# First loads in strict order, and the memory norm moved from the first to the second pass, in a two-layer encoder

## The chip, the cores and the metric

The kernel runs on all eight cores of one Trainium2 chip. Every core does the whole network for one of the eight batch elements, and no data passes between cores. The metric is device time in microseconds (us) of the slowest core. Cores 0 to 3 lie on one die, cores 4 to 7 on the other.

Executions come in two states. In the slow one a die, or both, shows a lower granted TensorE clock in the records, and the time is some per cent longer; the same kernel has both. One more disturbance turned up that this division into states doesn't catch: in some runs called fast, a *pair* of cores has a mean clock of 0.980 to 0.985 where the other cores have 0.992 and more, and the time is 12 to 28 us longer. The ratios on record count such runs as fast; each one is marked below.

Engine names: PE is TensorE (matmul), PEld its weight loads, DVE VectorE, ACT ScalarE, POOL GpSimd, SP SyncE. A name with q, as SPq, is an engine's sequencer, here the issue of a DMA.

## The reference, cut to what matters

```python
def rms_norm(x, g):
    y = x * lax.rsqrt(jnp.mean(x * x, axis=-1, keepdims=True) + EPS)
    return y * g

def swiglu(x, w_gate, w_up, w_down):
    return (jax.nn.silu(x @ w_gate) * (x @ w_up)) @ w_down

def reference(x, mem, ...):                  # x (8, 2048, 1024), mem (8, 256, 1024)
    for l in range(2):
        g = norm_g[l]
        h = swiglu(rms_norm(x, g[0]), ...)   # hidden width 2816: first FFN
        x = x + 0.5 * rms_norm(h, g[1])
        ...                                  # token mixer
        m = rms_norm(mem, mem_norm_g[l])     # the "memory norm"
        h = cross_attention(rms_norm(x, g[4]), m, ...)
        ...                                  # and a second FFN
    return x
```

The memory norm depends on `mem` alone, so it may be done at any time before the first cross-attention, some 600 us into the program. It is done once for both layers: they share the root mean square and differ in the gain.

## The kernel before: the parts that matter

A core's x is 2048 tokens in four blocks of 512 (x block 0 to 3, 2 MB each in fp32). An FFN makes two passes, each over two blocks: gate and up products first (11 pairs of hidden tiles), then the down-projection. The products are done with a seven-product Strassen scheme, for which VectorE makes sums of weights (tiles `SW`) and of inputs (tiles `TX`); in the down-projection these are `SDA` and `TS`. `ER` and `ss` are intermediate results, and `H` is the hidden result of a pair. Only the first two pairs of the first pass are done "plainly", with eight products in place of seven, because the input sums need x block 1, which isn't there yet. Weights come in panels of 256 KB through POOL's DMA queue (`SL<-wflat`), x and mem through SP's queue.

First loads and first products:

```python
k.dma("pool", ... CB ...)                       # a constant table
x_load(0, 2)                                    # x block 0, four DMAs
x_load(1, 4)                                    # x block 1, two DMAs, at once behind it
...                                             # panel 0 is issued when half of x block 1 is in:
reads=([("X", c, 1) for c in range(4)] if i == 0 else ())
...
for tb in tbs:                                  # plain products: block 0, pairs 0 and 1,
    for i in range(j0 // 2):                    # then block 1, pairs 0 and 1
        plain_pair(held[i], i, tb)
        if tb == tbs[1]:
            for nm in BLK:
                ws.release(held[i][nm])         # frees slots: the next panels can be issued
```

The rest of the first pass is a list of events at product steps (one step is eight matmuls of 128x512, about 1.7 us). x blocks 2 and 3 are issued from step 2, their norms come at steps 11.5 and 18.5, and the memory norm at step 21.5:

```python
if (l, f, hf) == (0, 0, 0):
    ev += [(XA + XD * n, "xload", ...) for n in range(8)]
    ev += [(XL[0], "xnorm", 2), (XL[1], "xnorm", 3), (XL[2], "mnorm", 0)]
```

```python
def mem_norm():
    k.later(None, writes=m32k, dma=("sp", [... m32 <- memT ...]))       # 1 MB
    k.later({"act": ... activation(out=msq, in_=m32, func=AF.Square)})  # one big square on ACT
    for c in range(8):
        stat_later(st, psk, MSQ[:, c, :], ..., n=MEM)                   # 8 matmuls: column sums
    rk_, use = rstd_later(...)                                          # ACT: Ln, then Exp(-0.5 *)
    for l in range(L):
        for c in range(8):                                              # 16 DVE operations
            ... scalar_tensor_tensor(out=MNL[l][:, c, :], in0=M32[:, c, :], scalar=gain, in1=R) ...
        ... DMA mscr[l] <- MNL[l] ...                                   # stored for the attention
```

The SwiGLU needs the function Silu on ACT, the norm needs Ln and Exp; this will matter.

The softmax here doesn't subtract the row's maximum and nothing guards it: scores larger than these inputs give would overflow.

## Time and profile before

| | before |
|---|---|
| time, the runs given at first | 2461.39 us median of 3 (2457.8 to 2772.29) |
| cores in the profiled run | 2434.2 to 2461.5 us, core 5 the slowest |
| PE busy, core 5 | 2373.9 us, 96% |
| first down-projection begins, by core | 171.2 us (core 6) to 190.5 us (core 3) |

The head of the profile's page, on core 5. The rows of digits are busy tenths in 40 slices of 61.5 us; PEclk is the granted clock in tenths.

```profile
span 2461.5 us, 35363 instructions; the slowest of 8 cores (2434.2 to 2461.5 us)
...
PE 2373.9 (96%) x11280; PEld 1094.8 (44%) x11280; DVE 1754.1 (71%) x2253; ACT 1229.2 (50%) x1757; POOL 352.6 (14%) x679
...
PE   6979999998999999999999999999999999999998
...
PEclk9989999999999999999999999999999999999999
```

What the reader is to see is that PE is the limit and that the only slices with a digit under 8 are the first (0 to 62 us) and the third (123 to 185 us). The view of waits tells what. It lists, for core 5 in the first 225 us, what PE stood for: the total, how often, and the longest, in us.

```profile
PE pp L350 <- ACT XN L930: 13.0, 4, 9.8
PE pp L350 <- ACT msq L2114: 11.3, 1, 11.3
PE pp L350 <- DMA SL<-wflat: 5.2, 2, 4.4
PE pp L350 <- ACT ER_76 L1282: 3.1, 1, 3.1
PE pp L350 <- DVE SW_80 L1260: 1.7, 1, 1.7
...
```

The first line is mostly the very start, where the first x has to land (9.8 us at one time). The second is the memory norm. The timeline of core 5 shows it; columns are start, duration, engine, line, operation and tiles, how many, and in brackets the idle time before and what ended it.

```profile
142.09 0.37 SPq L2112 DMA_DIRECT2D m_166<-memT  x1
...
162.47 1.91 ACT L2114 ACTIVATE msq<-m_166 128x2048 bf16<-128x2048 f32 x1 [13.32 <-DMA m_166<-memT]
...
164.63 1.65 PE L350 MATMUL pp<-msq,onesm 128*128 128x256 bf16 x7 [11.27 <-ACT msq L2114]
```

mem (its tile is `m_166`) is issued at 142.1 and lands 20 us later. ACT stands still for 13.3 us before the square (the bracket of its line): what is queued behind the square waits too, and PE with it for 11.3 us. In the view of windows the 20 us before and after the landing look like this (PE, PEld, DVE, ACT, POOL busy, then clock, DMA share, GB/s):

```profile
140.00:160.00 20.00, 13.33 (x62) 5.67 (x59) 10.68 (x13) 5.03 (x5) 2.63 (x5) 0.90 1.02 178
160.00:180.00 20.00, 15.31 (x63) 6.88 (x64) 9.25 (x14) 10.08 (x10) 0.00 (x0) 0.76 0.08 14
```

The DMA engines are full while mem lands, since weight panels go through them at the same time, and the clock is at 0.76 after the pause. The landing took 8.6 to 20.2 us over the cores, and the cores where it was long (0, 3, 4, 5 and 7: 14.6 to 20.2) are the cores that start their down-projection late (185.3 us and later).

### The profile page before, as it was taken

What the parts mean: (1) busy time and instruction counts of PE and PEld (TensorE: products, weight loads), DVE (VectorE), ACT (ScalarE), POOL (GpSimd) and SP (SyncE); (2) the same over time, 40 slices, a digit from 0 to 9 for tenths busy, and PEclk for the clock granted to TensorE, in tenths of its full rate; (3) what the DMA queues carried; (4) which work ended last, traced back from release to release, by engine and by line L of the source; (5) the groups of instructions that cost most, each with busy time, mean ns of one, the idle gap of its engine ahead of it and who ended that gap; (6) DMA issues with size and microseconds to landing.
All of it is one profiled execution on the core that took longest, in us unless ns stands there. A gap on an engine that the chain in (4) does not pass through costs nothing.

```text
span 2461.5 us, 35363 instructions; the slowest of 8 cores (2434.2 to 2461.5 us)
## 1 busy us (share of the span) xinstructions
PE 2373.9 (96%) x11280; PEld 1094.8 (44%) x11280; DVE 1754.1 (71%) x2253; ACT 1229.2 (50%) x1757; POOL 352.6 (14%) x679
## 2 busy tenths in 40 slices
PE   6979999998999999999999999999999999999998
PEld 2434444444454444444444444445444444444445
DVE  4656796566378888588679759836656878876765
ACT  3543553438667754365355345433227785634433
POOL 1111111112220011111111111111001101111210
PEclk9989999999999999999999999999999999999999
DMA  7755666758761167466666667675235204755954
GB/s 140 144 87 97 121 126 123 156 118 132 134 103 27 22 112 139 80 132 114 134 125 126 124 124 147 118 151 128 46 73 90 52 1 73 151 94 91 166 95 138
DMA packets 127684, 267.95 MB, mean 109 GB/s; under 512 B 15120, under 2 KB 25616, under 8 KB 127504
## 3 DMA queue, kind: packets, MB, share of 16 engines
q0 software_dynamic: 95760, 183.25, 47.1%
q1 hardware_dynamic: 31744, 82.44, 10.4%
q8 instruction: 96, 1.57, 0.3%
q14 instruction: 84, 0.69, 0.1%
HBM read 408.73 MB, written 35.91 MB: 181 GB/s over the span
## 4 chain that ended last, share of the span: by engine, by line
PE 85%; DMA 4%; DVE 4%; ACT 3%; issue 3%; SPq 1%; DVEq 0%; ACTq 0%; POOL 0%; POOLq 0%
PE pp L350 85%; DMA X<-xT 1%; DMA m_166<-memT 1%; DMA SL<-wflat 1%; SPq L1869 0%; DVE H L1284 0%; DMA mscr<-mnl_169 0%; ACT ER_76 L1282 0%; DMA slot_51<-wflat 0%; DMA slot_49<-wflat 0%; ACT rw L1087 0%; DMA YB<-YP_118 0%; ACT L1282 0%; DVE X L973 0%; ACT ER_77 L1282 0%
## 5 line engine op out<-in xcount | busy, mean ns | idle before, releaser
L350 PE MATMUL pp<-XH,SL 128*128 128x512 f16 x2192 | 493.9, 380 | 7.2 <-DMA SL<-wflat 5.2
L628 POOL DMA_DIRECT2D SL<-wflat x352 | 185.9, 531 | 1099.4 <-PE pp L350 807.9
L350 PEld LDWEIGHTS pp<-XH,SL 128*128 128x128 f16 x2192 | 213.8, 98 | 271.6 <-issue 19.1
L1401 ACT ACTIVATE X<-pp 128x512 f32<-128x512 f32 x112 | 66.9, 597 | 238.6 <-PE pp L350 232.1
L350 PE MATMUL pp<-TX_74,SL 128*128 128x512 f16 x688 | 163.1, 380 | 4.5 <-ACT ER_76 L1282 3.4
L350 PE MATMUL pp<-TX_72,SW_80 128*128 128x512 f16 x688 | 165.0, 382 | 1.8 <-DVE SW_80 L1260 1.7
L350 PE MATMUL pp<-XH,SW_79 128*128 128x512 f16 x688 | 163.8, 381 | 1.7 <-DVE ER_77 L1284 1.5
L350 PE MATMUL pp<-TX_73,SW_78 128*128 128x512 f16 x688 | 162.8, 379 | 0.9 <-DVE SW_78 L1260 0.9
L350 PE MATMUL pp<-XN,WQK 128*128 128x512 bf16 x512 | 121.2, 379 | 3.7 <-ACT VWO L1151 2.3
L930 ACT ACTIVATE XN<-X 128x512 bf16<-128x512 f32 x176 | 105.8, 638 | 35.6 <-DVE X L973 14.1
L1282 ACT ACTIVATE pp<-pp 128x1024 f32<-128x1024 f32 x86 | 86.7, 1008 | 40.1 <-PE pp L350 38.4
L1405 DVE TENSOR_TENSOR X<-pp,X 128x512 f32<-128x512 f32 x56 | 38.6, 690 | 95.1 <-PE pp L350 55.1
L350 PEld LDWEIGHTS pp<-TX_74,SL 128*128 128x128 f16 x688 | 66.5, 98 | 88.6 <-issue 10.3
L350 PEld LDWEIGHTS pp<-TX_72,SW_80 128*128 128x128 f16 x688 | 67.3, 98 | 85.2 <-issue 6.7
L350 PEld LDWEIGHTS pp<-XH,SW_79 128*128 128x128 f16 x688 | 67.1, 98 | 85.3 <-issue 6.9
L350 PEld LDWEIGHTS pp<-TX_73,SW_78 128*128 128x128 f16 x688 | 66.8, 98 | 83.5 <-issue 3.6
L1282 ACT ACTIVATE ER_77<-pp 128x1024 f32<-128x1024 f32 x61 | 62.2, 1020 | 55.5 <-PE pp L350 39.2
L1282 ACT ACTIVATE ss_81<-pp 128x1024 f32<-128x1024 f32 x60 | 61.2, 1020 | 53.3 <-PE pp L350 34.0
L1282 ACT ACTIVATE ER_75<-pp 128x1024 f32<-128x1024 f32 x62 | 63.2, 1020 | 44.8 <-PE pp L350 30.8
L1282 ACT ACTIVATE ER_76<-pp 128x1024 f32<-128x1024 f32 x61 | 62.2, 1020 | 45.9 <-PE pp L350 30.0
L945 DVE SCALAR_TENSOR_TENSOR XH<-X,cf_sb,rw 128x512 f16<-128x512 f32 x96 | 66.8, 746 | 20.8 <-PE pp L350 16.2
L350 PE MATMUL pp<-H,sdb 128*128 128x512 f16 (+1 forms) x352 | 78.8, 372 | 0.0
(663 smaller groups left out, 4603.4 us busy)
## 6 DMA issues: line engine op xcount, KB each, us to landing
SL<-wflat POOLq DMA_DIRECT2D x352, 256.0 KB, 5.4
xscr<-X SPq DMA_DIRECT2D x48, 512.0 KB, 4.0
X<-xscr SPq DMA_DIRECT2D x48, 512.0 KB, 4.9
WN_147<-wflat POOLq DMA_DIRECT2D x32, 352.0 KB, 6.0
X<-xT SPq DMA_DIRECT2D x20, 512.0 KB, 8.1
WSL<-wflat POOLq DMA_DIRECT2D x28, 352.0 KB, 11.1
WN_148<-wflat POOLq DMA_DIRECT2D x24, 352.0 KB, 7.1
wx_146<-wflat POOLq DMA_DIRECT2D x16, 352.0 KB, 6.7
```

What stands on the lines that cost most here:

```text
L350: self.q["pe"].append((waits, (lambda e: e.matmul(out, lhsT=l_, rhs=r_, start=st, stop=sp, skip_group_check=grp)), inc))
L628: self.k.dma("pool", lambda e, dst=dst, src=src: e.dma_start(out=dst, in_=src), "w%d" % idx, cost=1.6, reads=([("X", c, 1) for c in range( ...
L930: k.later({"act": lambda e, sap=sap, xap=xap: e.activation(out=sap, in_=xap, func=AF.Square)}, reads=[xk(c, tb)], writes=skeys)
L945: k.later({"dve": lambda e, c=c, oap=oap, xap=xap: e.scalar_tensor_tensor(out=oap, in0=xap, scalar=G(l, n, c), in1=R[st["r"]][:, :], op0=A ...
L1282: act = lambda o_, i_, fn, rk, wk, **kw: k.later({"act": lambda e: e.activation(out=o_, in_=i_, func=fn)}, reads=rk, writes=wk, cost={"act ...
L1401: cpy = lambda o_, b, wk, **kw: k.later({"act": lambda e: e.activation(out=o_, in_=P[b][:, 0:T], func=AF.Copy)}, reads=[("P", b)], writes= ...
L1405: k.later({"dve": lambda e: e.tensor_tensor(out=o_, in0=P[b][:, 0:T], in1=o_, op=ALU.add)}, reads=[("P", b)] + ok, writes=ok, **kw)
```

## The change

The intent is to give the opening a strict order of loads, so that the first product starts early and nothing that isn't wanted yet takes bandwidth, and to take the memory norm out of a stretch where its load comes late. x is also laid out by block in memory, so that a load of a block reads long runs. The core of the diff (cut are the layout of x, the constant table `CB`, which is now loaded late, the split of `plain_pair` into products and evacuation, six filler matmuls behind the first pair, and the squares of x block 1, which are now summed by eight matmuls instead of by VectorE and two):

```diff
-        x_load(0, 2)
-        x_load(1, 4)
+        for c in range(0, 8, 2):
+            x_part(0, c, 2)
+        ws.prefetch(4, [xk(4, 0)])                       # panels 0-3 behind 3/4 of x block 0
+        for c in range(0, 8, 2):
+            x_part(1, c, 2, w_key(2) if c == 0 else ())  # x block 1 behind panel 2
+        ws.prefetch(8, [xk(4, 1)])                       # panels 4-7 behind 3/4 of x block 1
+        for tb in (2, 3):
+            for c in (4, 6, 0, 2):
+                x_part(tb, c, 2, w_key(6) if (tb, c) == (2, 4) else ())   # x 2, 3 behind panel 6
...
-                    for tb in tbs:
-                        for i in range(j0 // 2):
+                    for i in range(j0 // 2):
+                        for tb in tbs:                   # pair 0: block 0, block 1; then pair 1
+                            made = plain_pair(held[i], i, tb)
...
+                        if i == 0:                       # third pair: its weight sums, early
+                            ps[j0 // 2] = Pair(l, f, hf, j0 // 2)
+                            ps[j0 // 2].sums()
...
-        XL = (11.5, 18.5, 21.5)
+        XL = (11.5, 18.5)
+        ML = (43.5, 59.5)
...
-                    ev += [(XA + XD * n, "xload", (2 + n // 4, (4, 6, 0, 2)[n % 4])) for n in range(8)]
-                    ev += [(XL[0], "xnorm", 2), (XL[1], "xnorm", 3), (XL[2], "mnorm", 0)]
+                    ev += [(XL[0], "xnorm", 2), (XL[1], "xnorm", 3)]
+                if (l, f, hf) == (0, 0, 1):              # second pass
+                    ev += [(ML[0], "mload", 0), (ML[1], "mnorm", 0)]
...
-                stat_later(st, psk, MSQ[:, c, :], msqk, c == 0, c == 7, n=MEM)
+                stat_later(st, psk, MSQ[:, c, :].unsqueeze(1).broadcast_to([128, 2, MEM]), msqk, c == 0, c == 7)
```

The norm's tiles move with it: from the place of x blocks 2 and 3, which is free in the first pass once those are normalised, to that of blocks 0 and 1, which is free in the second pass once those are spilled.

More of the change, by code (lines that the diff above doesn't have):

```diff
@@ L83, in to_phase, with pack_x @@
     return np.ascontiguousarray(a.reshape(a.shape[0], PW, NPH).transpose(0, 2, 1)).reshape(a.shape[0], S)
+def pack_x(x):
+    return np.ascontiguousarray(to_phase(np.ascontiguousarray(x.T)).reshape(8, 128, NTB, TB).transpose(2, 1, 0, 3))
 def from_phase(a):
@@ L616, in __init__, with prefetch, _issue @@
         self.wflat = None
-    def _issue(self):
+    def prefetch(self, n, gate):
+        while self.sched is not None and self.issued < n:
+            self._issue(gate)
+            gate = ()
+    def _issue(self, gate=()):
         i = self.issued
@@ L628, in _issue @@
         self.k.dma("pool", lambda e, dst=dst, src=src: e.dma_start(out=dst, in_=src), "w%d" % idx, cost=1.6,
-                   reads=([("X", c, 1) for c in range(4)] if i == 0 else ()), writes=keys)
+                   reads=gate, writes=keys)
         self.issued += 1
@@ L697, in build @@
     nc = bass.Bass("TRN2", target_bir_lowering=False)
-    xT = nc.dram_tensor("xT", [D, S], F32, kind="ExternalInput").ap()
+    xT = nc.dram_tensor("xT", [NTB, 128, 8, TB], F32, kind="ExternalInput").ap()
     memT = nc.dram_tensor("memT", [D, MEM], F32, kind="ExternalInput").ap()
@@ L785, in build @@
     TSR = sb("tsr", OFF_X + 30720, [NK - 9, TU], F16)
-    M32 = sb("m32", OFF_X + 32768, [8, MEM], F32)
-    MSQ = sb("msq", OFF_X + 40960, [8, MEM], BF16)
-    MNL = [sb("mnl%d" % i, OFF_X + 45056 - i * 4096, [8, MEM], BF16) for i in range(L)]
+    M32 = sb("m32", OFF_X, [8, MEM], F32)
+    MSQ = sb("msq", OFF_X + 8192, [8, MEM], BF16)
+    MNL = [sb("mnl%d" % i, OFF_X + 12288 - i * 4096, [8, MEM], BF16) for i in range(L)]
     WQK = AT(nc, "WQK", 32768, [8, 1024], BF16)
@@ L824, in program @@
         k.dma("sp", lambda e: e.dma_start(out=CF[:, :], in_=cfd), "c0", writes=[("CF",)])
-        k.dma("pool", lambda e: e.dma_start(out=CB[:, :], in_=cbd), "c1", writes=[("CB",)])
-        xv = xT.rearrange("(c p) t -> p c t", p=128)
+        k.t["hq"] = 4.0
         def x_part(tb, c, n, reads=()):
@@ L830, in x_part, with w_key @@
             k.dma("sp", lambda e: e.dma_start(out=X[:, lo // 1024, c:c + n, lo % 1024:lo % 1024 + TB],
-                                              in_=xv[:, c:c + n, lo:hi]), "xl%d_%d" % (tb, c),
+                                              in_=xT[tb, :, c:c + n, :]), "xl%d_%d" % (tb, c),
                   reads=reads, writes=[xk(q, tb) for q in range(c, c + n)], cost=0.9 * n)
-        def x_load(tb, n):
-            for c in range(0, 8, n):
-                x_part(tb, c, n)
-        x_load(0, 2)
-        x_load(1, 4)
+        def w_key(i):
+            return SLOTS16[i]((0, SLOT_ELEMS))[1]
+        for c in range(0, 8, 2):
[7 more added lines that the diff above has]
+                x_part(tb, c, 2, w_key(6) if (tb, c) == (2, 4) else ())
         k.op("dve", lambda e: e.memset(ONESM[:, :], 1.0 / 1024.0), writes=[("ONES",)])
@@ L845, in program @@
         k.op("dve", lambda e: e.memset(SGN[:, 1:2], -isq), writes=[("ONES",)])
-        CONST = [("CF",), ("CB",), ("ONES",)]
+        CONST = [("CF",), ("ONES",)]
+        CONSTB = CONST + [("CB",)]
         k.op("act", lambda e: e.activation(out=SS[0][:, 0:2], in_=ONES1[:, 0:2], func=AF.Ln), reads=[("ONES",)], writes=[("S", 0)],
@@ L909, in add @@
                     self.stack.append((sq, sqk))
-        stats = {}
+        stats, rks = {}, {}
         k.sqfree = list(range(7))
@@ L941, in prenorm @@
             stats[(l, n, tb)] = psk
+            rks[(l, n, tb)] = rk_
             for c in (4, 5, 6, 7, 0, 1, 2, 3) if n in (0, 6) and tb > 1 else range(8):
@@ L1215, in x_reload @@
             lo, hi = p * 2 * TB, (p + 1) * 2 * TB
-            src = xv[:, c, lo:hi] if (l, f) == (0, 0) and hf == 0 else xscr[:, c, lo:hi]
+            src = xT[2 * p:2 * p + 2, :, c, :].rearrange("t p n -> p t n") if (l, f) == (0, 0) and hf == 0 else xscr[:, c, lo:hi]
+            dst = X[:, p, c, :].rearrange("p (t n) -> p t n", t=2) if (l, f) == (0, 0) and hf == 0 else X[:, p, c, :]
             k.later(None, reads=[("XS", c, p)] + list(paced), writes=[xk(c, 2 * p), xk(c, 2 * p + 1)], dma=("sp", [
-                lambda e: e.dma_start(out=X[:, p, c, :], in_=src)], "xs%d_%d" % (p, c), 3.0))
+                lambda e: e.dma_start(out=dst, in_=src)], "xs%d_%d" % (p, c), 3.0))
         def ho_x(tb):
@@ L1473, in plain_pair @@
             lo, hi = tbr(tb)
-            tl = ((tb % 2) * TB, (tb % 2 + 1) * TB)
             tiles = [(q, r) for q in range(2) for r in "12"]
@@ L1482, in plain_pair, with plain_evac @@
                     k.mm(P[b][:, :], [(w.t[:, o:o + 128], xap, w.keys + xkeys)], b, start=(kk == 0), stop=(kk == 7))
+            return i, tb, bs
+        def plain_evac(i, tb, bs):
+            tl = ((tb % 2) * TB, (tb % 2 + 1) * TB)
             for q in range(2):
@@ L1494, in program @@
         RB = (2.2, 5.2, 7.2, 10.2, 14.2, 16.2, 18.2, 20.2)
-        XA, XD = 2.0, 1.7
-        XL = (11.5, 18.5, 21.5)
+        XL = (11.5, 18.5)
+        ML = (43.5, 59.5)
         MORE = 2
@@ L1511, in ffn @@
                 plain = nxt is None and hf == 1
+                ps = {}
                 j0 = 0
@@ L1520, in ffn @@
                         k.mm(P[b][:, :], [(ONESM[:, :], ALT[:, :], [("ONES",), stats[(0, 0, 0)]])], b)
-                    for tb in tbs:
-                        for i in range(j0 // 2):
-                            plain_pair(held[i], i, tb)
-                            if tb == tbs[1]:
-                                for nm in BLK:
-                                    ws.release(held[i][nm])
+                    for i in range(j0 // 2):
+                        for tb in tbs:
+                            made = plain_pair(held[i], i, tb)
+                            if (i, tb) == (0, 0):
+                                b = k.bank()
+                                for _ in range(6):
+                                    k.mm(P[b][:, :], [(ONESM[:, :], ALT[:, :], [("ONES",)])], b)
+                                k._check([rks[(0, 0, 1)]] + [q for kk in range(4) for q in XH(kk, tbr(1))[1]], [])
+                            plain_evac(*made)
+                        for nm in BLK:
+                            ws.release(held[i][nm])
+                        if i == 0:
+                            ps[j0 // 2] = Pair(l, f, hf, j0 // 2)
+                            ps[j0 // 2].sums()
                     token_sums(0, 2)
@@ L1530, in ffn @@
                 ev = [(7 * (i - i0) + first.get((i - i0, pr), off), pr, i) for i in range(i0, i1)
-                      for pr, off in (PLAN if i < i1 - 1 else PLANQ)]
+                      for pr, off in (PLAN if i < i1 - 1 else PLANQ) if i not in ps or pr not in ("in", "sum")]
                 end = 7 * (i1 - i0)
                 if (l, f, hf) == (0, 0, 0):
-                    ev += [(XA + XD * n, "xload", (2 + n // 4, (4, 6, 0, 2)[n % 4])) for n in range(8)]
-                    ev += [(XL[0], "xnorm", 2), (XL[1], "xnorm", 3), (XL[2], "mnorm", 0)]
+                    ev += [(XL[0], "xnorm", 2), (XL[1], "xnorm", 3)]
+                if (l, f, hf) == (0, 0, 1):
+                    ev += [(ML[0], "mload", 0), (ML[1], "mnorm", 0)]
                 if (l, f, hf) != (0, 0, 0) and not plain:
@@ L1567, in ffn @@
                 ev.sort(key=lambda x: x[0])
-                ps = {}
                 k.wide, k.lag = True, LAG
@@ L1576, in ffn @@
                         ps[i].last()
-                    elif pr == "xload":
-                        x_part(i[0], i[1], 2, tick())
                     elif pr == "xnorm":
@@ L1582, in ffn @@
                         k.bg = False
+                    elif pr == "mload":
+                        k.later(None, reads=tick(), writes=[("CB",)], dma=("pool", [lambda e: e.dma_start(out=CB[:, :], in_=cbd)], "c1", 1.6))
+                        mem_fetch(tick())
                     elif pr == "mnorm":
@@ L1702, in even_mixer @@
                 b = k.bank()
-                k.mm(P[b][:, :], [(CB[:, CB_CSC + j * 128:CB_CSC + (j + 1) * 128], CB[:, CB_FW:CB_FW + 512], CONST)], b)
+                k.mm(P[b][:, :], [(CB[:, CB_CSC + j * 128:CB_CSC + (j + 1) * 128], CB[:, CB_FW:CB_FW + 512], CONSTB)], b)
                 oap = CW.h[:, j, :, :].rearrange("p g d -> p (g d)")
@@ L1823, in stats @@
                     def stats(r=r, yh=yh, yhk=yhk, y2=y2, y2k=y2k):
-                        k.mm(P[st["m"]][:, :], [(BO, yh, yhk + CONST)], st["m"], start=(r == 0), stop=(r == 3), main=False)
-                        k.mm(P[st["v"]][:, :], [(BO, y2, y2k + CONST)], st["v"], start=(r == 0), stop=(r == 3), main=False)
-                    k.later(None, reads=yhk + y2k + CONST, writes=[psk], pre=pre, mm=stats)
+                        k.mm(P[st["m"]][:, :], [(BO, yh, yhk + CONSTB)], st["m"], start=(r == 0), stop=(r == 3), main=False)
+                        k.mm(P[st["v"]][:, :], [(BO, y2, y2k + CONSTB)], st["v"], start=(r == 0), stop=(r == 3), main=False)
+                    k.later(None, reads=yhk + y2k + CONSTB, writes=[psk], pre=pre, mm=stats)
                 return i, st, psk, ys, gr, grk
@@ L2105, in odd_mixer, with mem_fetch @@
             out_proj(lambda c: ("lin", "od_w_out", 0, c), rhs, 8, l, n_post, False, nxt)
+        xk2 = lambda *cs: [xk(c, tb) for c in cs for tb in (0, 1)]
+        def mem_fetch(paced):
+            m32, m32k = M32[:, :, :], xk2(0, 1)
+            k.later(None, reads=paced, writes=m32k, dma=("sp", [lambda e: e.dma_start(out=m32, in_=memT.rearrange("(c p) m -> p c m", p=128))], "ml", 4.0))
         def mem_norm():
-            xk2 = lambda *cs: [xk(c, tb) for c in cs for tb in (2, 3)]
             m32, m32k = M32[:, :, :], xk2(0, 1)
@@ L2111, in mem_norm @@
             mnk = [xk2(3), xk2(2)]
-            k.later(None, writes=m32k, dma=("sp", [lambda e: e.dma_start(out=m32, in_=memT.rearrange("(c p) m -> p c m", p=128))], "ml", 4.0))
             k.later({"act": lambda e: e.activation(out=msq, in_=m32, func=AF.Square)}, reads=m32k, writes=msqk, cost={"act": 2.0})
@@ L2289, in program @@
         prenorm(0, 0, 0, False)
-        prenorm(0, 0, 1)
+        prenorm(0, 0, 1, False)
         for si, (kind, l, f, n_pre, n_post) in enumerate(subs):
@@ L2359, in run @@
         in_maps.append({
-            "xT": to_phase(np.ascontiguousarray(inp["x"][b].T)),
+            "xT": pack_x(inp["x"][b]),
             "memT": np.ascontiguousarray(inp["mem"][b].T),
```

## The prediction

> **What bounds it now.** TensorE: busy 2373.9 of 2461.5 us (96%); the chain that ended last is 85% PE. Only the opening differs much between cores. I split each core's span at its first down-projection matmul of the first pass (timeline by core): before it lie 171.2 us (core 6) to 190.5 us (core 3); after it all cores take 2263 to 2272 us. Core 5, the slowest: 189.1 + 2272.4. The change touches the opening only.
>
> **Losses there, core 5 (waits and timeline).**
> 1. First product at 24.5 us (22.4 to 25.8 over the cores): weights are issued at 18.6, after half of x block 1, and PE waits for them (5.2 us in all).
> 2. 33 us for four plain pairs, 128 matmuls of 0.216 us = 27.6 us of work, then 1.7 us behind a DVE sum.
> 3. 3.1 us at 80 us, less near 92 us: ScalarE, in order, stands behind squares whose x blocks 2 and 3 come late.
> 4. Memory norm: memT takes 20.2 us to land (8.6 on core 6), its square blocks ScalarE's queue, PE waits 11.3 us, then runs cold (clock 0.76 in 160 to 180 us): some 13 us. Cores 0, 3, 4, 7 wait 5.8 to 8.2 us, cores 1, 2, 6 at most 0.8. memT lands slowly beside weight panels (DMA share 1.02 in 140 to 160 us). The Trainium skill, "DMA: Bandwidth & Descriptors", Queues, rings and completion order, says that each engine takes turns between its queues; this agrees. The clock agrees with "TensorE: Matmul & The Clock Gate", Part 1: an idle window of about 3.4 us throttles.
>
> **What the change does.**
> - Item 4 goes: memT is fetched in the second pass, 16 product steps of 1.73 us = 27.6 us (estimate) before use; its slowest landing was 20.2. Its 16 DVE operations of 0.48 us and one ACT of 1.9 us fit there (DVE 0.8 to 0.9, PE 1.00 busy in 280 to 400 us). Added: stat matmuls twice as wide, 8 x 0.108 = 0.9 us. Worth 13 us on core 5, 8 to 13 on 0, 3, 4, 7, about 0 on 1, 2, 6.
> - Item 3 goes: x blocks 2 and 3 are issued near 40 us, not 60 to 80: 2 to 5 us.
> - Items 1 and 2: four panels are issued once 3/4 of block 0 is in (near 13.5 us), so the first product comes near 20 us. But x block 1 waits for the third panel (near 22 us), lands near 30, and its products start near 34: a gap of some 6 us after the first pair. Three pairs of 6.9 us follow: the plain part ends near 56, against 57.5 now. x blocks 2 and 3 then compete with panels 8 to 11, wanted near 57: 0 to 3 us lost. Net gain 0 to 3 us.
>
> So the down-projection should begin at 168 to 174 us on every core, and the slowest core end near **2440 us** (-0.9%), range **2429 to 2451**. Chances: faster by over 2% 0.03, within 2% 0.95, slower 0.02.
>
> **What would show it.** No PE wait behind the memory square; cores within about 12 us of each other (27 now); first product near 20 us, a gap behind it that ends on XH of block 1; no ScalarE wait on x after 60 us; the rests after the split unchanged within 3 us.
>
> **What would make it wrong.** The late panels starving behind x blocks 2 and 3 (a PE wait for SL near 57 to 65 us); the norm's square stalling ScalarE again in the second pass; the mscr write holding back the second down-projection; a start that gains much more than I allow.

## The result, and the profile after

| | before | after |
|---|---|---|
| median, runs on the same chip | 2463.28 us of 4 (fast: 2457.8, 2461.39, 2465.18) | 2455.53 us of 4 (2453.53 to 2456.36, all fast) |
| ratio of the fast runs | | 0.9978, 95% interval 0.9962 to 0.9994 |
| profiled run, slowest core | 2461.5 us (core 5) | 2455.0 us (core 2) |
| profiled run, mean of the cores | 2449.8 us | 2447.4 us |
| profiled run, cores apart | 27.3 us | 13.7 us |

Ratios in this text use fast runs alone, so they are not the ratio of the medians (the median before has the slow run of 2772.29 in it). The means of the fast runs are 2461.5 and 2455.2 us. The change is worth 0.2%, some 6 us: within 2% as foretold, and faster, but less than a third of the 21 us predicted, and outside the predicted range of 2429 to 2451.

The page's head after, on core 2. The third slice of the PE row is no longer weak. The spans of the cores, in its first line, have drawn together, from 27 to 14 us, but from both ends: the best core is 7 us slower than the best before.

```profile
span 2455.0 us, 35391 instructions; the slowest of 8 cores (2441.3 to 2455.0 us)
...
PE 2378.8 (97%) x11292; PEld 1094.2 (45%) x11292; DVE 1752.1 (71%) x2250; ACT 1231.6 (50%) x1759; POOL 353.0 (14%) x679
...
PE   7999999998999999999999999999999999999998
...
PEclk9999999999999999999999999999999999999999
```

The waits of PE in the first 225 us, on core 2, after (the lines cut are of 1.5 us and less):

```profile
PE pp L353 <- ACT XN L944: 12.6, 8, 8.8
PE pp L353 <- DVE H L1508: 3.5, 1, 3.5
PE pp L353 <- DVE XH L960: 2.5, 1, 2.5
...
```

The square is gone, and so is the wait for ER of 3.1 us (items 4 and 3 of the prediction). The window of 140 to 160 us, with full DMA engines as before, now has a busy PE at full clock:

```profile
140.00:160.00 20.00, 20.00 (x95) 9.00 (x94) 13.79 (x16) 8.02 (x8) 4.19 (x8) 1.00 0.94 161
```

To see where the gain went I cut each core's timeline at the first matmul of each stage (the second pass at its first TX product, 1.9 us after its very first matmul; the mixer at its first matmul with a weight slot). Mean of the eight cores, us; in brackets PE's idle time (the gaps between matmuls) in that stage:

```
stage                                          before            after             change
start to first product                          23.99 [ 5.99]     17.05 [1.49]      -6.9
plain products, to first Strassen TX product    35.10 [ 2.81]     44.53 [8.13]      +9.4
Strassen products of the first pass            123.21 [11.06]    110.97 [1.76]     -12.2
down-projection of the first pass               69.54 [ 0.88]     68.94 [0.41]      -0.6
products of the second pass                    133.08 [ 0.38]    137.25 [2.45]      +4.2
down-projection of the second pass              67.52 [ 0.46]     70.71 [3.24]      +3.2
(sum: the mixer begins at)                     452.45            449.45             -3.0
from there to the end                         1997.32           1997.92             +0.6
```

Two parts speak against the prediction, and both grew: the plain part, and the second pass. In the plain part 5.3 of the 9.4 us are idle time; most of the rest are matmuls that stand in this stage now, eight for the statistics of x block 1 (two before) and five or six fillers (none before). On the slowest cores the sum is plain. Core 5 before: 189.1 us to its first down-projection, then 2272.4. Core 2 after: 175.8, then 2279.2. So the opening gained 13.3 us and the rest lost 6.9.

**The second pass.** The waits of PE between 240 and 450 us. First core 5 before (the line cut is of 0.2 us, as in the two fences of this kind that follow):

```profile
PE pp L350 <- DVE SDA L1379: 0.4, 1, 0.4
...
```

Core 2 after:

```profile
PE pp L353 <- ACT X L1417: 2.4, 2, 1.7
PE pp L353 <- ACT pp L1298: 1.5, 1, 1.5
PE pp L353 <- DVE SDA L1395: 1.0, 1, 1.0
...
```

The timeline of core 2 after shows what stands behind the wait for `ACT pp`, and behind the longer of the two for `ACT X`:

```profile
355.56 1.28 ACT L879 ACT_TABLE_LOAD   x1 [4.40 <-DVE XN L1144]
356.86 0.38 ACT L879 ACTIVATE rw<-pp 128x256 f32<-128x256 f32 x1
357.33 1.01 ACT L1298 ACTIVATE pp<-pp 128x1024 f32<-128x1024 f32 x1
358.36 1.28 ACT L1298 ACT_TABLE_LOAD   x1
358.49 1.89 PE L353 MATMUL pp<-TX_73,SW_78 128*128 128x512 f16 x8 [1.53 <-ACT pp L1298]
359.66 1.06 ACT L1298 ACTIVATE ss_81<-ss_81 128x1024 f32<-128x1024 f32 x1
...
361.64 1.28 ACT L882 ACT_TABLE_LOAD   x1
362.94 0.42 ACT L882 ACTIVATE rw<-rw 128x256 f32<-128x256 f32 x1
...
364.02 1.28 ACT L1298 ACT_TABLE_LOAD   x1 [0.66 <-DVE mnl_168 L2155]
...
395.37 0.32 SPq L2159 DMA_DIRECT2D mscr<-mnl_169  x1
...
400.12 2.53 PE L353 MATMUL pp<-TS_140,SDA 128*128 128x512 f16 x11 [0.96 <-DVE SDA L1395]
...
403.12 1.09 ACT L1417 ACTIVATE X<-pp 128x512 f32<-128x512 f32 x2 [6.15 <-DMA mscr<-mnl_169]
404.35 1.89 PE L353 MATMUL pp<-TS_142,wx_145 128*128 128x512 f16 x8 [1.70 <-ACT X L1417]
```

A Silu (359.66) stands between the norm's Ln (356.86) and its Exp (362.94). ACT therefore loads the tables for Ln, for Silu, for Exp and for Silu again, 1.28 us each. The 16 DVE operations end long after that: the last `mnl_169` is done when the down-projection has begun, its store `mscr<-mnl_169` is issued at 395.4, and the new residual, which goes where the norm's tiles stand, can't be written before that store has read them. That is the 1.7 us at 404.35. The other wait for `ACT X`, 0.7 us at 396.6, is released by the last `mnl_169` itself, and the one for `SDA`, 1.0 us, comes from VectorE, which has no idle time before it between 386 and 400 us and still does four of the norm's operations there. All three go back to the norm's coming late; only the first is the store's. The Trainium skill, "ScalarE: Activation LUTs", Table sets: the hidden batching unit, says to batch activations by table set, and that Ln followed by Exp needs one load since both are in one set. The trace agrees, and shows the other side of it: with a Silu between them it is four.

**The plain part.** The timeline of core 2 after, from the first product on:

```profile
16.87 0.38 PE L353 MATMUL pp<-XH,SL 128*128 128x512 f16 x1
18.72 6.85 PE L353 MATMUL pp<-XH,SL 128*128 128x512 f16 x31 [1.47 <-DMA SL<-wflat]
...
25.84 1.15 ACT L944 ACTIVATE XN<-X 128x512 bf16<-128x512 f32 x2 [10.24 <-DMA X<-xT]
...
36.05 23.79 PE L353 MATMUL pp<-XH,SL 128*128 128x512 f16 x100 [2.48 <-DVE XH L960]
...
60.42 0.69 DVE L1276 TENSOR_TENSOR SW_80<-SL 128x1024 f16<-128x1024 f16 x1 [11.25 <-DMA SL<-wflat]
...
63.33 1.12 PE L353 MATMUL pp<-XH,SL 128*128 128x512 f16 x4 [3.48 <-DVE H L1508]
```

The first product is 7 us earlier than before. But the first quarter of x block 1 is there only at 25.8, and the block's first product starts at 36.05, 10.5 us after the last product of pair 0 on block 0 (it starts at 31 to 36 us over the cores); between them PE has only the statistics of block 1 and fillers. PE comes out of this gap at a granted clock of 0.50 (36 to 40 us on core 2; its first nine products are 0.43 us apart and not 0.216, some 1.9 us in all). Then the weight sum `SW_80`, which now stands first in VectorE's queue, waits for panels 8 to 11 until 60.4 us, and `H`, which would free PE's banks, waits behind it.

### The profile page after: what moved, and what is told of

It is laid out like the page before. It is cut to its first block, busy times and chain, and to the rows that moved or that the text cites. A ratio compares the mean times of both kernels' runs of the same rounds, so it can differ in the third digit from the quotient of the medians.

```text
span 2455.0 us, 35391 instructions; the slowest of 8 cores (2441.3 to 2455.0 us)
## 1 busy us (share of the span) xinstructions
PE 2378.8 (97%) x11292; PEld 1094.2 (45%) x11292; DVE 1752.1 (71%) x2250; ACT 1231.6 (50%) x1759; POOL 353.0 (14%) x679
## 4 chain that ended last, share of the span: by engine, by line
PE 86%; DVE 3%; DMA 3%; ACT 3%; issue 3%; SPq 0%; DVEq 0%; POOL 0%; ACTq 0%; POOLq 0%
PE pp L353 86%; DMA SL<-wflat 1%; DMA X<-xT 1%; DMA slot_46<-wflat 0%; SPq L1898 0%; DMA mscr<-mnl_169 0%; DVE H L1300 0%; DMA YB<-YP_118 0%; ACT rw L1102 0%; ACT ER_77 L1298 0%; DMA slot_48<-wflat 0%; DVE X L988 0%; DVE SDA L1395 0%; ACT ER_76 L1298 0%; DVE TT_138 L2068 0%
```

## The experiments

Three theories about the missing gain, with the words that abbreviate them:

- the memory-norm theory: moving the norm is what shortens the first pass's products, and it is paid in the second pass, by ScalarE's table loads and the late store;
- the load-order theory: it is the new loads that matter, for both; with x blocks 2 and 3 early, mem would land fast even where it was, and the second pass suffers from something else the change brings;
- the late-panel theory: at the start, what the early first product gains is lost because panels 8 to 11 stand behind 4 MB of x blocks 2 and 3.

### First set: a chip in the slow state

The first four kernels went to a chip where every run, those of the kernel before included (2652 to 2832 us), was in the slow state or so near it that the clock was 0.90 to 0.92 on the worse cores. Nothing of time can be read there. They were the same edits as some of those below, and one more.

`e1_mem_back`: the norm put back into the first pass, the rest of the change kept (edit: see e5).

> The changed kernel, but the memory norm again in the first pass (new first loads kept). Theory M, the moved norm itself costs the second pass: the stretch from the first product of the second pass to the end of its down-projection (208.0 us mean over the cores in the changed kernel, 200.6 before) falls back to 200 to 201 us, and the products of the first pass (111.0 us) grow to 114 to 125 us with a PE wait behind the memory square. Rival R, the longer second pass comes from what else moved there (x reload in halves, the constant load): it stays at 207 to 208 us. Slowest core by M: 2452 to 2460 us.

Measured: 2649.0 us median (2647.04 to 2654.12), against 2657.5 for before.

`e2_mem_only`: the kernel before with nothing but the norm moved (edit: see e6).

> The kernel before, with only the memory norm moved into the second pass (first loads as before). M: first product and plain part unchanged (24 and 59 us), products of the first pass 123.2 to 112-115 us, second pass 200.6 to 207-208 us, cores within 12 us of each other, slowest core 2450 to 2456 us, so most of what the whole change gains. R: the second pass stays near 200.6 and the slowest core ends near 2443 to 2447 us.

Measured: 2656.82 us, against 2657.5.

`e3_mem_early`: the changed kernel with the norm 16 steps earlier in the second pass (edit: see e7).

> The changed kernel with the memory norm 16 steps (27 us) earlier in the second pass (spills of x closer together, so that the space is free). If the second pass lost its 7.4 us because the norm comes too late, next to the start of the down-projection (X blocked until the norm's store has landed) and with its logarithm and exponential split by the SiLU: second pass 208.0 to 202.5-204 us, the down part alone 70.7 to 67.5-68.5 us, slowest core 3 to 5 us faster. If the norm's own work costs it wherever it stands: second pass stays at 206 us or more.

Measured: 2664.1 us.

`e4_sums_late`: the changed kernel without the early weight sums of the third pair.

```diff
-                        if i == 0:
-                            ps[j0 // 2] = Pair(l, f, hf, j0 // 2)
-                            ps[j0 // 2].sums()
```

> The changed kernel without the early weight sums of the first Strassen pair (they come at their old place in the plan). Theory S, the sums stand in VectorE's queue before the products of the plain pairs while panels 8 to 11 are late: the PE wait of 2.1 to 3.5 us on H goes, the first Strassen product of the second kind (61.6 us mean) starts at 59.5 to 61 us. Rival: the late panels alone set it, and it stays at 61 to 62 us.

Measured: 2656.64 us. PE's idle time in the plain part was 6.8 us (mean of the cores; 8.1 in the changed kernel on the good chip), but at this low clock the waits are shorter in other kernels too (e1 idles 2.9 us in the first pass's products; e5 below, the same kernel on a better chip, 8.3 us on its six undisturbed cores). On the same chip e1 and e3, which keep the early sums, idle 6.7 and 5.3 us in the plain part, and the part ends at 62.1 and 61.7 us, in e4 at 61.7. No gain is seen: on core 2 the wait for H is gone and one of 1.8 us for the weight sum SW stands in its place. The rival that was named, that the late panels alone set the end, fits; at this clock it is not settled.

One thing could be read even here, since it doesn't depend on small differences: PE's idle time in the second pass (products plus down-projection) was 0.7 us in e1, where the norm is gone from there, 2.7 in e2, where only the norm is there, and 0.2 in e3, where it is there earlier. It pointed to the memory-norm theory. The set was repeated on another chip.

### e5_mem_back: the norm back in the first pass

```diff
-    M32 = sb("m32", OFF_X, [8, MEM], F32)            # and MSQ, MNL likewise
+    M32 = sb("m32", OFF_X + 32768, [8, MEM], F32)
-                    ev += [(XL[0], "xnorm", 2), (XL[1], "xnorm", 3)]
+                    ev += [(XL[0], "xnorm", 2), (XL[1], "xnorm", 3), (21.5, "mnorm", 0)]
-                        mem_fetch(tick())            # in the second pass
...
+                        mem_fetch([])                # directly before mem_norm(), first pass
                         mem_norm()
```

> The kernel of e1 again, because that chip granted a clock of 0.87 to 0.95 in the opening. Theory M: second pass back to 200 to 201 us (208.0 in the changed kernel), PE idle in it 0.7 us (5.7). New question from e1: with x blocks 2 and 3 early, memT may land in time even in the first pass. If so (theory L, the early loads and not the move cure the stall), PE idle in the first pass's products stays at 2 to 4 us mean (11.1 before, 1.8 changed), and the slowest core ends 3 to 6 us before the changed kernel, near 2450 us. If the move is needed, idle there is 8 us or more.

Measured: 2466.41 us median (2458.19 to 2479.3), ratio to before 1.0026 (0.9972 to 1.0079). In two of the four runs, the profiled one among them, a pair of cores had a clock of 0.983; I leave cores 2 and 3 of the profile out for the first pass. The waits of PE in the first 225 us, on core 5 (the longest alone):

```profile
PE pp L353 <- ACT msq L2146: 12.3, 1, 12.3
...
```

The wait is back, at its old size, with the new loads in place. On the six undisturbed cores mem took 8.3 to 21.6 us to land, and the first pass's products took 120.9 us (111.1 on the same six cores of the changed kernel). The second pass took 200.6 us on the mean of the cores, exactly what it took before (200.6), against 208.0 with the change.

What follows: the load-order theory falls on both counts. The new loads don't cure the landing of mem, and the second pass loses its 7.4 us with the norm and with nothing else.

### e6_mem_only: the kernel before with only the norm moved

```diff
-                    ev += [(XL[0], "xnorm", 2), (XL[1], "xnorm", 3), (XL[2], "mnorm", 0)]
+                    ev += [(XL[0], "xnorm", 2), (XL[1], "xnorm", 3)]
+                if (l, f, hf) == (0, 0, 1):
+                    ev += [(43.5, "mload", 0), (59.5, "mnorm", 0)]
...                                    # tiles, fetch and wide sums as in the change
```

> The kernel of e2 again at a full clock. M: second pass 200.6 to 206-208 us, first pass's products 123.2 to 113-116 us (PE idle 11.1 to about 4 us, what stays are the late x blocks), plain part unchanged at 59 us, slowest core 2450 to 2456 us.

Measured: 2461.52 us median; fast runs 2458.73, 2460.97 and 2461.52, one with a pair of cores at 0.981 at 2486.76, and one slow. Ratio 1.0031 (0.9949 to 1.0113), which includes the run with the disturbed pair. The first pass's products took 115.5 us (123.2 before), the second pass 208.55 us (200.60 before). The slowest core was expected at 2450 to 2456 us; that was missed. The waits of PE between 240 and 455 us, on core 2 (cut are lines of 0.5 us and less):

```profile
PE pp L350 <- ACT X L1401: 2.5, 2, 1.9
PE pp L350 <- ACT pp L1282: 1.5, 1, 1.5
PE pp L350 <- DVE SDA L1379: 1.0, 1, 1.0
...
```

What follows: the three waits of the changed kernel's second pass appear, with their sizes, in a kernel that has none of the new loads. The norm's move alone takes 7.7 us from the products of the mean core's first pass and gives 8.0 back in the second pass (208.55 less 200.60); the mean core gains nothing (the mixer begins at 451.9 us, 452.5 before). The remaining shortening of the first pass's products in the changed kernel, from 115.5 to 111.0, goes with the early x blocks 2 and 3: on core 2 e6 still has a wait of 3.8 us for ER, behind a square for which ACT waits 4.5 us for x, and the changed kernel has none.

### e7_mem_early: the norm 16 steps earlier in the second pass

```diff
-        ML = (43.5, 59.5)
+        ML = (29.5, 43.5)
-                    ev += [(7 * n + 7.5, "spill", c) for n, c in ...]
+                    ev += [((3.5 if (l, f, hf) == (0, 0, 1) else 7) * n + 7.5, "spill", c) for n, c in ...]
```

The second line frees the place for mem earlier: x is spilled at twice the rate in this one pass.

> The kernel of e3 again at a full clock; e3 had 0.3 us of PE idle in the second pass at a low clock. If lateness is the cause: second pass 208.0 to 202-203.5 us with under 1 us idle, slowest core 2448 to 2452 us. If the norm's own work costs it: 206 us or more.

Measured: 2466.29 us median; the two runs without a disturbed pair took 2451.71 and 2457.29, the two with one (0.982 to 0.985) 2475.29 and 2477.21. Ratio 1.0017 (0.995 to 1.0083), all four counted. The second pass took 203.3 us (208.0 with the norm where the change put it), its down-projection 67.1 us with no idle time to speak of (0.03 us, against 3.24). Its products took 136.2 us (137.3) with 1.5 us of idle time (2.45); under 1 us was expected for the whole pass, so that was missed. The waits of PE between 240 and 450 us on core 2:

```profile
PE pp L353 <- DVE ER L1300: 1.7, 1, 1.7
PE pp L353 <- DVE X L1421: 0.5, 1, 0.5
...
```

What follows: the loss in the second pass is one of place, most plainly in the down-projection. On core 2 the last store is issued at 378.7 us, 0.3 us after the down-projection's first matmul; in the changed kernel it is 395.4, 13.9 us after it. In the products the wait for `ACT pp` is gone on all cores, and here the norm's Ln and Exp met without a Silu between them. But much of that gain is taken back: on seven of the eight cores PE waits 0.4 to 2.5 us for `ER` of VectorE, on core 2 behind a weight sum that stands 2.2 us for its panel (`SL<-wflat`). So core 2's products take 136.7 us in both kernels. Between 250 and 445 us the trace of core 2 has 6 table loads in the kernel before, 10 in the changed kernel, and 7 here and in e12 below, where the norm stands as early. Four more loads of 1.28 us are 5.1 us of ACT; PE waits for a part of them only.

### e8_x1_free: x block 1 no longer held behind the third panel

```diff
-            x_part(1, c, 2, w_key(2) if c == 0 else ())
+            x_part(1, c, 2)
```

> The changed kernel with x block 1 issued right behind block 0, no longer held until the third weight panel has landed. Theory G, the hold makes the gap of some 10 us after the first plain pair: the first product comes later (17.1 to 18-21 us), the gap shrinks to under 4 us, and the first Strassen product of the second kind starts at 56 to 59 us instead of 61.6. Rival B, the opening is bound by the bytes (4 MB of x and 4 MB of weights) whatever their order: it stays at 61 to 62 us.

Measured: 2456.92 us median (2453.89 to 2459.09, four fast runs), ratio 0.9981 (0.996 to 1.0003): as good as the changed kernel. The first product came at 21.3 us (17.05), and the plain part ended at 59.6 us (61.6; before 59.1), between the two ranges expected, 56 to 59 and 61 to 62. The gap is gone: PE idles 3.4 us in the plain part on core 2, where it was 10.2. The waits of PE in the first 225 us on core 2 no longer have a line for XH, which took 2.5 us, and have a longer one for the panels:

```profile
...
PE pp L353 <- DMA SL<-wflat: 4.4, 2, 3.1
PE pp L353 <- DVE H L1508: 2.1, 1, 2.1
...
```

What follows: holding x block 1 wins 4.3 us at the first product and loses 6.2 after it. As part of the order of loads it is worth minus 2 us at the end of the plain part; 2.6 to 5.6 were expected.

### e9_after_again: the changed kernel unchanged, a control

> The changed kernel once more, unchanged, so that the next three are compared with it on the same chip. All theories: 0.996 to 1.000 of the kernel before, stages as first seen (mean over cores: first product 17 us, first TX product 61.6, first down-projection 172.6, second pass 208.0).

Measured, on a third chip: two fast runs, 2456.78 and 2476.0 (the second with a pair of cores at 0.985), and two slow ones. The stages repeat within 0.7 us on the mean of the cores: first product at 17.15, plain part 45.2 (44.5), first pass's products 110.8, second pass 208.0.

### e10_x23_after: x blocks 2 and 3 held until panel 11

```diff
-        for tb in (2, 3):
-            for c in (4, 6, 0, 2):
-                x_part(tb, c, 2, w_key(6) if (tb, c) == (2, 4) else ())
...
                         if i == 0:
+                            for tb in (2, 3):
+                                for c in (4, 6, 0, 2):
+                                    x_part(tb, c, 2, w_key(3) if (tb, c) == (2, 4) else ())
```

(The slot of panel 3 holds panel 11 by then.)

> The changed kernel with x blocks 2 and 3 held until weight panel 11 has landed instead of panel 6. Theory P, panels 8 to 11 take 10 us and more beside these 4 MB and PE waits for what is queued behind them: the wait on H (2.1 to 3.5 us) goes, the first TX product starts at 58.5 to 60 us instead of 61.6, and blocks 2 and 3 still come before ScalarE needs them (products of the first pass stay within 1.5 us of 111.0). Rival: the panels are late for another reason; 61 to 62 us stays.

Measured: 2458.03 us median (2455.78, 2455.88, 2460.19, and 2483.87 with a pair at 0.98, which was the profiled run), ratio 1.0005 (0.9936 to 1.0074). For the first pass I read cores 0 to 5 only, which are undisturbed there, and beside them the same cores of the changed kernel. The plain part ended at 58.0 us (61.6; 62.3 in e9 on this chip). The first pass's products then took 113.1 us, with 4.3 us of idle time (110.9 and 1.7); within 1.5 us of 111.0 was expected, so that was missed. On core 2 of this run the view of waits no longer has a wait for H of the plain part, and has one for a weight sum after it:

```profile
...
PE pp L353 <- DVE SW L1273: 3.9, 1, 3.9
...
```

What follows: the late-panel theory names a real cost, 3.6 us at the start. But of these 2.2 are given back in the products that follow, and the same wait has only moved: on core 2 panels 8 to 11 now land 4 to 6 us after their issue (9 to 14 in the changed kernel), but panels 12 to 15, issued from 54.8 us beside x blocks 2 and 3, take 8 to 15 us, and at 73.7 us a weight sum has waited 4.7 us for the last of them. The 1.4 us that remain are too few for the times to show.

### e11_best: e7, e8 and e10 together; and e12_mem_only_early: the kernel before with only the norm moved, and moved early

e11 has the three edits above. e12 is e6 with e7's numbers:

```diff
-                    ev += [(43.5, "mload", 0), (59.5, "mnorm", 0)]
+                    ev += [(29.5, "mload", 0), (43.5, "mnorm", 0)]
...                                    # and the spills of that pass 3.5 steps apart
```

> Together: x block 1 not held, x blocks 2 and 3 after panel 11, memory norm 16 steps earlier in the second pass. If the terms add: first TX product at 56.5 to 58.5 us, first down-projection at 167 to 170 us, second pass 203 to 203.5 us; mean over the cores some 8 us under the changed kernel, slowest core 2442 to 2449 us.

> The kernel before with only the memory norm moved, but 16 steps earlier in the second pass than the change has it. If lateness was the whole fault of the move: second pass 208.5 (e6) to 203 to 204 us, first pass as in e6 (24, 59, 174 us), mean over cores some 4 us under the kernel before, slowest core 2449 to 2456 us. What e11 has beyond this is what the order of the first loads is worth.

Measured, both with only two fast runs each:

| | fast runs, us | ratio to before | first product | plain part ends | first pass's products | second pass | mixer begins |
|---|---|---|---|---|---|---|---|
| e11 | 2451.71, 2451.8 | 0.9956 (0.993 to 0.9981) | 21.2 | 57.5 | 113.8 | 203.5 | 443.8 |
| e12 | 2450.72, 2450.69 | 0.9951 (0.9926 to 0.9977) | 24.7 | 60.1 | 114.8 | 202.4 | 446.2 |
| changed kernel | 2453.53 to 2456.36 | 0.9978 (0.9962 to 0.9994) | 17.05 | 61.6 | 111.0 | 208.0 | 449.5 |

The waits of PE between 240 and 450 us on core 2 of e12 hold no ACT X, no ACT pp and no SDA any more:

```profile
PE pp L350 <- DVE X L1405: 0.5, 1, 0.5
PE pp L350 <- ACT ER L1282: 0.2, 1, 0.2
...
```

And its timeline has Ln and Exp behind a single table load:

```profile
351.07 1.28 ACT L865 ACT_TABLE_LOAD   x1
...
352.36 0.39 ACT L865 ACTIVATE rw<-pp 128x256 f32<-128x256 f32 x1
...
353.76 0.41 ACT L868 ACTIVATE rw<-rw 128x256 f32<-128x256 f32 x1
```

e11 missed what was expected of it, except for its plain part and its second pass: the first down-projection begins at 171.4 us on the mean of the cores (167 to 170), the mean of the cores is 5 us under the changed kernel's (8), the slowest core at 2451.7 (2442 to 2449). e12 came out as expected or better: second pass 202.4 us (203 to 204), the mean of the cores 6.2 us under the kernel before (4), the slowest core at 2450.7 (2449 to 2456).

What follows: e12, which has one of the change's two parts and puts it at a better place, is about 0.5% under the kernel before, and its mixer begins 3.3 us earlier than the changed kernel's. The intervals of the two ratios overlap, so that it beats the changed kernel is likely rather than settled; on the same chip the changed kernel's undisturbed fast run took 2456.78 us. The new order of loads isn't needed for it. e11 starts its mixer 2.4 us earlier than e12 and is still not faster: the mean of its cores ends at 2442.3 us (2443.6 in e12), but its slowest core, core 1, takes 82.0 us where the mean of e12's cores takes 79.0, in the stage before the mixer's output product, and 73.7 against 72.1 in the next, up to the attention's first product on x. These two stages vary by 3 to 5 us between the cores in the profiles of the kernel before, the changed kernel, e11 and e12.

## Why the prediction was right or wrong

The direction and the class (within 2%) were right, the size was not: 21 us foretold, 6.2 us measured between the means of the fast runs. For the slowest core of the profiled run the miss can be written as a sum. The prediction of 2440 took core 5's rest of 2272.4 us as unchanged, so it allowed 167.6 us for the opening. Core 2 had 175.8 and 2279.2. Of the 15.0 us by which it came later, 8.1 are the opening and 6.9 the rest.

**Item 4, the wait for the memory square: right.** e6 and e5 show it from both sides. With the norm gone, the first pass's products are 7.7 us shorter on the mean (e6); with the norm put back under the new loads, PE waits 12.3 us for the square on core 5 (e5). The drop to a clock of 0.76 goes with it: in the window of 160 to 180 us the changed kernel has 1.00 on core 2.

**"The rests after the split unchanged within 3 us": wrong; this is the first step that failed.** The rest grew by 7.4 us on the mean of the cores (2267.5 to 2274.8) and all of that is in the second pass. The prediction charged 0.9 us, for stat matmuls twice as wide. The matmuls cost 1.7 us there, because all eight (8 x 0.216 us), not only the added halves, moved into this pass: in the first pass they had been part of the opening. PE's idle time there grew by 4.9 us (0.84 to 5.69), in two pieces: waits in the products, next to the table loads that Ln and Exp cause when a Silu comes between, and waits in the down-projection, for the norm's last operations on VectorE and for the store that holds the place of the new residual. (1.7 and 4.9 make 6.6 of the 7.4 us; the rest isn't accounted for.) I had counted the norm's operations and seen that they fit into the busy shares of DVE and PE. Busy shares say that there is room, not in which order an engine's queue meets the work. I had named both (the square stalling ScalarE, the store holding back the second down-projection) under what would make the prediction wrong, and given them no microseconds. That the norm is the cause is shown by e6 (it brings the cost alone), e5 (without it the cost is gone) and e7 (moved earlier, 4.7 us of it are gone). That the down-projection's part is due to the norm's coming late is shown by e7 and e12, where its last store is issued as the down-projection begins and the idle time of 3.2 us falls to nothing; that the store itself is 1.7 us of it on core 2 is read from the timeline, and no run moves the store alone. How much of the products' part is due to the table loads isn't separated from the square and the wide matmuls in the same stretch: e7 and e12 moved them all, and in e7 a late panel takes much of the gain back. No run has a norm without Ln and Exp.

**Items 1 and 2, "the plain part ends near 56": wrong; the second step that failed.** It ended at 61.6 us on the mean and at 64.3 on core 2, 8.3 us late, which is about that core's whole miss in the opening. The first product was better than foretold (17.05, foretold 20). The gap after the first pair was mis-sized: foretold as 6 us, it was 10.5 on core 2, because x block 1 arrived, by quarters, from 25.8 us to 31.6 and its statistics come only after the last; the slow clock behind the gap, some 1.9 us there, was left out of "three pairs of 6.9 us". e8 puts the price of holding the block at 2 us net. The wait at the end of the plain part, foretold as 0 to 3 us, was 3.5 on core 2, and e10 shows that panels standing behind x blocks 2 and 3 cost 3.6 us there, 2.2 of which came back as a later wait for panels when these blocks were held. A full gain of 0 to 3 us for items 1 and 2 was foretold; it was a loss of 2.5.

**Item 3, x blocks 2 and 3: right in kind and size.** The waits for ACT behind squares are gone, and the first pass's products are 4.5 us shorter than in e6, where only the norm moved (foretold 2 to 5). In e10, where these blocks come later, no such wait returns; its 2.2 us more are a wait for panels.

**The cores within about 12 us of each other: right** (13.7). The opening now begins its down-projection at 169.2 to 175.8 us over the cores (foretold 168 to 174; before 171.2 to 190.5). This is where the gain of the metric comes from. The mean core gained 2.4 us, the slowest 6.5, because the cores with late mem were the slow ones.

**Left open.** In every fast profile the cores of a pair (0 and 1, 2 and 3, ...) differ (by 8 to 19 us before, by 3 to 11 after, by 9 to 12 in e12), and a part of it arises in the stages around the mixer's output and the attention, where often one core of a pair takes longer than the other (in e12 73.7 and 70.8 us for cores 0 and 1 before the attention). The Trainium skill, "HBM Reference", Specifications (TRN2), says that two cores share a domain's bandwidth; that would fit, but no run here tests it.

## What to carry to other kernels

Work that is moved into a "full" but smooth stretch has to be checked against the order of the work in each engine's queue there: which functions it puts between which (a table load each way), which buffer it holds, and when that is wanted next; free shares of busy time don't answer this. Move a prologue item as early into the new stretch as its buffer allows, so that its last store is done before the next stage needs the place; here the same norm 16 steps earlier was worth 4.7 us (e7) and 6.2 us (e12 against e6) in the second pass. And an order of loads that brings the first product forward is worth only what the second and the third product don't give back: sum the stage, not its first event.

## What the Trainium skill lacked or had wrong

- "ScalarE: Activation LUTs", What ACT_TABLE_LOAD costs: it gives about 1283 ns for the load and 1380 ns for a drain, 2.66 us for each switch. The load measured 1.28 us here as well, but the drain doesn't show: between the end of the activation before it and the start of the one behind it lie 1.3 us (an activation ends at 361.63 us, the load runs from 361.64, the Exp starts at 362.94). Half the page's figure is what a switch cost ACT.
- "DMA: Bandwidth & Descriptors", Queues, rings and completion order: it tells that the engines take turns between queues, and the trace agrees, but no page says what a bulk load pays for it. Here 1 MB on SP's queue beside 256 KB panels on POOL's took 8.3 to 21.6 us in the first pass (e5, undisturbed cores) and 6.0 to 8.5 us in the second (the changed kernel). A range of this kind next to the mechanism would have been of use.
- "TensorE: Matmul & The Clock Gate", Part 1: it says that once three cores of a die run dense matmuls the whole die goes to 13/16 of the clock, and advises to budget with that for all-core work. In the fast profiles of the kernel before and of the changed kernel all eight cores keep a mean granted clock of 0.993 to 0.998 with PE 96 to 97% busy, so the budget is too low for them. A clock of 0.81 did occur: for a whole die over a whole slow run (cores 0 to 3 of e9's third run, 0.812 to 0.814, 2907 us), which agrees with the page, and for a pair of cores in runs called fast (cores 6 and 7 of e10, 100 to 180 us: 0.81, with cores 4 and 5 of the same die at 1.00; cores 2 and 3 of e5 likewise 0.81, then 0.96 in the next 120 us, then 1.00). The page doesn't tell that the same kernel runs with and without it, and no page tells of a throttle of a pair; here it costs 12 to 28 us of the metric.
